# A decoder step on one core: low halves at the bottom of the mix's pool, raw weights in an empty weight place, and rooms of their own for norm and forget values

## The chip, the cores and the metric

One core of a Trainium2 chip. The metric is the device time of one execution in microseconds; each kernel is run several times, and the median counts.

## The reference, cut to what matters

One layer of a hybrid decoder for 512 prompt tokens and 8 sequences of 8 new tokens, D = 1024, all in float32:

```python
mod = einsum('bd,de->be', silu(c), w_ada) + b_ada            # six rows: sh1 sc1 gt1 sh2 sc2 gt2
h = rms_norm(x, norm1_g) * (1 + sc1) + sh1
z = einsum('btd,dc->btc', h, w_in)                           # queries, keys, values, forget, gates mg
...                                                          # two attentions: o_fox, o_nsa
mix = sigmoid(mg_fox) * (o_fox @ w_br_fox) + sigmoid(mg_nsa) * (o_nsa @ w_br_nsa)
x = x + gt1 * (mix @ w_out)
h = rms_norm(x, norm2_g) * (1 + sc2) + sh2
y = x + gt2 * (relu(h @ w_up) ** 2 @ w_down)
```

The forgetting attention adds a difference of summed log forget values to its scores. The sparse attention works on compressed keys, on 16 selected blocks and on a window. For the new tokens, keys, values and log forget values of 2048 past tokens come out of paged caches.

## The kernel before, in words

**Halves.** Each large product is made of three matmuls, high x high, low x high and high x low. `split` (L131) writes the high half with ACT, and the low half as a subtraction on DVE. `stream` (L169 to L184) brings a weight: SP issues the DMA of a raw piece (L179), then the piece is split into its high and low places. With raws=0 the raw piece takes a room of the pool praw, which all such weights share; it has 5 rooms of 4 KB per partition in the program before.

**Stages, in order of time.** The first stage (up to about 166 us) compresses the cached keys and values of the sparse attention in 40 units u, and beside them makes the first norm and the conditioning rows; what is done at which unit is written out by hand in lists (`todo[u]`, L592 ff.). `ada_first` is a conditioning product with a 1 MB weight tile (wada) that POOL loads; `cmp_pages` asks SP for cache pages (cpg); `stage_logf` and `store_logf` gather log forget values and store them again. Then come the projections (to about 305 us), which also leave the normed rows h, split into a high and a low half, in a buffer in DRAM (hfd), the prompt's attention (to about 455 us), the samples' attention (to about 606 us), the mix (to about 768 us), the output projection `out_part` (to about 829 us) and the MLP (8 blocks of an up and a down part).

**Samples' attention** (`sample_attention`, L1554 ff.). 32 units u, four for each sequence. A step of its loop turns the keys of unit u + 1 (`key_rows`: transposes k, then copies kt on ACT and DVE), makes the scores of unit u, and the values (so) of unit u - 3, the key and value rows being fr and sr tiles loaded by SP. forget_split and forget_turned make, once for each sequence, the transposed log forget sums DT out of DH, and E is a constant of selected ones; DH, DT and E stand in the pool sp, which the samples' attention opens when the pools of the prompt's attention close. At u = 24 the high halves hH of all rows are loaded from hfd by POOL. At u = 30 `mix_open` opens praw and asks for the first gate's weights, and in the last steps `mix_first` does the first gate's matmuls with hH. A list that is written out by hand (self.chain) keeps TensorE in program order there and in out_part.

**Mix** (`mix_part`, L1840 to L1916). For each of 8 column blocks e, and for x = 0, 1: a gate mg (8 pieces k of h, two halves of the columns, three matmuls, so 48), its tanh on ACT, and a branch br (4 pieces, 24 matmuls) out of the split attention output oH, oL. Before the first e, two gate results (mg0), oH and oL, the weights of e = 0, and then the low halves hL (16 DMAs on POOL, L1896 and L1897) are taken from the pool pq, in this order from the bottom. Pools give the same memory out again, from the bottom of the stack or, with side="right", from the other end; a tile waits for the last users of what stood at its place. SP then also loads the rows of x2 (L2187).

**Output and MLP.** out_part has four quarters of w_out (wo0 to wo3), each with a place (`place_of`) in pools pwt or pm, and goes through five row tiles i; the norm of a finished row tile (`norm_scaled`, ACT squares, DVE scales it into nsq) is turned by TensorE (`norm_parts`, nt) at a later point of a written-out list (turn_at). gate_prompt and gate_sample make the factors gp and gs. The last row tile's norm is made in mlp, in the room of the accumulator acc. The MLP's w_down halves (wd) use places w3 in pwt, and w0 in its own pool pf; its raw pieces are those of praw.

The order on each engine within what these lists leave open is set by a scheduler (schedule_with_timeline_sim). issue_after pins an instruction behind another in that order.

Of the kernel before, what the change touches and what calls it, by code (L numbers as in the profile page):

```python
# [45 lines left out]
class Step:  # L46
# [121 lines left out]

    def stream(self, pool, src, shape, tag, uid, raws=2, bufs=2, parts=2, room=None, pin=None):  # L169

        nc = self.nc
        wh, wl = room or [pool.tile(shape, F32R, tag=tag + c, bufs=bufs, name=f"{tag}{c}{uid}") for c in "hl"]
        n = shape[1] // parts
        for i in range(parts):
            s = slice(n * i, n * i + n)
            raw = (pool.tile([P, n] + shape[2:], F32, tag=tag + "r", bufs=raws, name=f"{tag}r{uid}_{i}") if raws else
                   self.praw.tile([P, n] + shape[2:], F32, tag="raw", bufs=5, name=f"{tag}r{uid}_{i}"))
            for sl, a in src(s):
                nc.sync.dma_start(raw[sl], a)  # L179
# [331 lines left out]
    def first_stage(self, pl, pe, hf, seam):  # L511
# [182 lines left out]
    def norm_scaled(self, sq, n, i, x, junk=None):  # L694

        t0, m = TILES[i]
        ss = self.small.tile([P, 1], F32, tag="nss", name=f"nss{n}_{i}")
        self.act((sq if junk is None else junk)[:m], x[:m], AF.Square, accum_out=ss[:m])
# [852 lines left out]
    def sample_attention(self, sp, sp0):  # L1551
        nc = self.nc
        self.E = sp.tile([P, 8, 64], F32R, name="E")
        self.tt(self.E, self.tok[:, :, None].to_broadcast([P, 8, 64]), self.hot[:, None, :].to_broadcast([P, 8, 64]), OP.mult)  # L1554
# [13 lines left out]
        for u in range(4 * NB + 4):  # L1568
# [92 lines left out]
    def forget_split(self, sp, b):  # L1661
        self.DH = DH = sp.tile([P, 2, 2, 64], F32R, tag="DH", bufs=1, name=f"DH{b}")
        for hf in range(2):
            d = self.Dt[:, b, 8 * hf:8 * hf + 8, :].rearrange("p c h -> p (c h)")
            self.act(DH[:, hf, 0, :], d)
            self.tt(DH[:, hf, 1, :], d, DH[:, hf, 0, :].bitcast(F32), OP.subtract)

    def forget_turned(self, sp, b):
        tb = self.mmb(f"dt{b}")
        for hf in range(2):  # L1670
            self.tr(tb[:, P * hf:P * hf + P], self.DH[:, hf].rearrange("p a n -> p (a n)").bitcast(F32))
        self.DT[b] = sp.tile([P, 2, P], F32R, tag="DT", bufs=2, name=f"DT{b}")
        self.cp(self.DT[b], tb[:, 0:256].rearrange("p (a n) -> p a n", a=2))
# [154 lines left out]
    def gate_weights(self, e, x):  # L1828
        return self.stream(self.pqr, self.cols(self.I["w_in"], TOK + D * x + P * e, P), [P, NK, P], "wm", f"{x}_{e}", raws=0, parts=1)

# [8 lines left out]

    def mix_part(self, pq, pr, pm, mix2):  # L1840
# [26 lines left out]
        def gate(e, x, w, ks=None):  # L1867
            t = pq.tile([P, NT], F32, tag="mgt", bufs=2, name=f"mgt{e}{x}") if e else mg0[x]
            if e + x == 0:
# [16 lines left out]
        def weights(e, x):  # L1886
            return (self.w0 if e + x == 0 else self.gate_weights(e, x),
                    self.stream(pq, br_src(x, e), [P, 4, P], "wb", f"{x}_{e}", raws=0, parts=1))

        with self.tc.issue_after(self.last_exp):  # L1890
            ws = [weights(0, x) for x in range(2)]

        hL = pq.tile([P, NK, NT], F32R, name="hL2")
        for k in range(NK):

            nc.gpsimd.dma_start(hL[:, k, 0:SEQ], self.hfd[:, k, NT + NS:2 * NT])  # L1896
            nc.gpsimd.dma_start(hL[:, k, SEQ:NT], self.hfd[:, k, NT:NT + NS])  # L1897
        for e in range(NK):
            if e == 0:
                for k in range(8):  # L1900
                    self.split(oH[:, k], oL[:, k], self.oT[:, k])
# [9 lines left out]
            if e == NK - 1:  # L1911
                self.wo0 = self.out_weights(0, self.place_of(0, "wo0", NK, pm))
            (nc.gpsimd if e < NK - 1 else nc.vector).tensor_tensor(m[0], m[0], m[1], op=OP.add)
# [12 lines left out]
    def gate_sample(self, pool, j0, scale, uid, room=None):  # L1926

        gx = room if room is not None else pool.tile([P, NK, NB, 8], F32, tag="gx", bufs=1, name=f"gx{uid}")
        self.cp(gx, self.modT[:, j0:j0 + NK, 1:9, None].to_broadcast([P, NK, NB, 8]))
# [7 lines left out]

    def place_of(self, n, uid, a, pool=None):
# [3 lines left out]
    def out_weights(self, q, room):  # L1942
        return self.stream(None, self.cols(self.I["w_out"], 256 * q, 256), [P, NK, 256], "wo", q, raws=0, room=room)

    def out_part(self, pw, mix2, x2, h3):
        nc, I = self.nc, self.I
        rooms = [self.place_of(q, f"wo{q}", NK) for q in (3, 2, 1)]
        ws = [self.wo0] + [self.out_weights(q, rooms.pop()) for q in range(1, 4)]
        self.shift = self.mod_coef(1)
        g = None  # L1950
        self.chain = ""

        rest, turn_at = {}, {(1, 1): 0, (2, 0): 4, (2, 3): 1, (3, 3): 2}
        for i in (0, 4, 1, 2, 3):
# [17 lines left out]
            if i != 3:  # L1972
                sq = pw.tile([P, D], F32, tag="nsq", bufs=1, name=f"nsq{i}")
                self.norm_scaled(sq, 1, i, x2[:, i])
                rest[i] = lambda i=i, sq=sq: self.norm_parts(i, h3, sq, pw.tile([P, 4, P], F32, tag="nv", bufs=1, name=f"nv{i}"))


    def mlp(self, pf, h3, x2, acc):
# [36 lines left out]

        self.norm_scaled(acc[:, 0], 1, 3, x2[:, 3])
        for blk in range(NBLK):
# [3 lines left out]
            for q in range(2):  # L2021
                v = I["w_down"][0, 512 * blk + 256 * q:512 * blk + 256 * q + 256, :].rearrange("(k p) c -> p k c", p=P)
                w = self.stream(None, lambda s, v=v: [((slice(None),), v[:, s])], [P, 2, D], "wd", f"{blk}{q}",
                                raws=0, room=self.place_of((3, 0)[q], f"wd{blk}{q}", 2, pf if q else None), pin=None if blk else self.normed)
                wd += [(w[0][:, k], w[1][:, k]) for k in range(2)]
# [35 lines left out]
    def run(self):  # L2061
# [46 lines left out]
        lctx.close()  # L2108
        op = self.pool("op2", octx)
        self.Dt = op.tile([P, NB, 16, 8], F32, name="Dt")  # L2110
# [71 lines left out]
        with ExitStack() as c:  # L2182
            c.push(self.mctx)
            self.mix_part(self.pool("pq", c), self.pqr, pm, mix2)
        x2 = keep.tile([P, 5, D], F32, tag="r1", bufs=1, name="x2")
# [5 lines left out]
        h3.append([h31[:, 0], h31[:, 1]])  # L2191
        self.pwt = self.pool("pwt", self.top, side="right")
        with ExitStack() as c:
            self.out_part(self.pool("pw2", c), mix2, x2, h3)
# [46 lines left out]
```

## Time and profile before

| | us |
|---|---|
| median of 3 runs | 1249.14 (1248.99 to 1249.55) |
| profiled execution | 1249.57 |
| span of its profile | 1247.7 |
| TensorE busy (PE) | 1194.9 |
| VectorE (DVE), ScalarE (ACT), GpSimd (POOL) busy | 687.6, 514.2, 127.1 |
| HBM traffic over the span | 166 GB/s |

How to read it: times in the profile are microseconds from the start of the span. A row of the waits names the waiting engine and tile, then what released it, then total, times and longest. A row of a timeline is start, duration, engine, line, operation, out<-in, shape, count, and in brackets the idle time before it and what ended it. A row of the chain is start, duration and what was under way, followed back from the last instruction. A row of windows has the window, its length, busy time and count of instructions in it for PE, its weight loads (PEld), DVE, ACT and POOL, and then the granted TensorE clock, the share of the DMA engines that was busy, and GB/s.

### The profile page before, as it was taken

How to read it: one execution, taken by the hardware profiler on the slowest of the kernel's cores; microseconds unless marked ns; L12 is line 12 of the kernel's file. 1: busy time of each engine (PE TensorE's matmuls, PEld its weight loads, DVE VectorE, ACT ScalarE, POOL GpSimd, SP SyncE). 2: the span in 40 equal slices, each digit the busy share in tenths (PEclk: the TensorE clock that was granted, in tenths of full speed). 3: DMA queues.
4: the chain of work that ended last, by engine and by line, in shares of the span. 5: the costliest groups of instructions: out<-in, count | busy, mean ns of one | idle time of the engine just before them, and what ended most of it. 6: DMA issues, size and time to landing. Idle time of an engine off the chain costs nothing.

```text
span 1247.7 us, 24815 instructions
## 1 busy us (share of the span) xinstructions
PE 1194.9 (96%) x9475; PEld 1024.9 (82%) x9475; DVE 687.6 (55%) x1875; ACT 514.2 (41%) x1152; POOL 127.1 (10%) x142
## 2 busy tenths in 40 slices
PE   3899999999999999999799999999999999999998
PEld 3877789998666556666699999998989889899896
DVE  4678775686788745655444345655333333424545
ACT  2454453454777744445332233365423223232230
POOL 1020100001211300000200000002102011020110
PEclk9999999999999899999899999999999999999999
DMA  9599556794866559786833342115314223142102
GB/s 209 163 259 248 153 151 227 242 321 139 282 225 182 168 191 320 243 276 214 218 87 89 88 119 88 49 52 153 101 34 136 68 69 101 46 124 69 51 1 76
DMA packets 170201, 188.11 MB, mean 151 GB/s; under 512 B 16185, under 2 KB 149762, under 8 KB 167906
## 3 DMA queue, kind: packets, MB, share of 16 engines
q1 hardware_dynamic: 157890, 167.13, 44.5%
q0 software_dynamic: 6880, 16.25, 4.6%
q10 hardware_dynamic: 5312, 3.15, 1.1%
q8 instruction: 75, 1.23, 0.4%
q14 instruction: 44, 0.36, 0.1%
HBM read 176.48 MB, written 30.90 MB: 166 GB/s over the span
## 4 chain that ended last, share of the span: by engine, by line
PE 82%; DMA 7%; DVE 5%; SPq 3%; ACT 2%; issue 1%; POOL 0%; DVEq 0%; ACTq 0%
PE dn L77 17%; PE up L77 16%; PE mg L77 8%; PE z L77 7%; PE br L77 4%; PE hid L77 4%; PE ss L77 4%; PE wo L77 4%; DMA cpg<-in_cache_nsa_kv 4%; SPq L155 2%; PE k L83 2%; PE so L77 2%; PE ct L83 1%; PE sp L83 1%; PE ada L77 1%
## 5 line engine op out<-in xcount | busy, mean ns | idle before, releaser
L77 PE MATMUL z<-winh,h 128*128 128x264 f32 (+1 forms) x576 | 111.0, 287 | 0.6 <-ACT winh L112 0.3
L77 PEld LDWEIGHTS z<-winh,h 128*128 128x128 f32 x576 | 91.7, 190 | 2.7 <-DVE h L774 0.9
L2011 POOL TENSOR_TENSOR u<-u 128x576 f32<-128x576 f32 x32 | 50.7, 1585 | 417.0 <-ACT u L112 319.0
L77 PE MATMUL z<-winl,h 128*128 128x264 f32 (+1 forms) x320 | 88.2, 284 | 0.5 <-DVE winl L131 0.5
L77 PE MATMUL mg<-hL,wmh 128*128 128x288 f32 x256 | 76.0, 309 | 8.0 <-DMA hL<-hfd 8.0
L100 DVE TENSOR_TENSOR acc<-acc,dn 128x512 f32<-128x512 f32 x60 | 39.8, 684 | 76.5 <-PE dn L77 76.5
L77 PE MATMUL mg<-hH,wmh 128*128 128x288 f32 x256 | 76.8, 301 | 0.0
L77 PE MATMUL mg<-hH,wml 128*128 128x288 f32 x256 | 76.0, 298 | 0.6 <-DVE wml L131 0.6
L112 ACT ACTIVATE xh<-ct 128x256 fp32r<-128x256 f32 x128 | 47.9, 384 | 59.0 <-PE ct L83 36.2
L774 DVE TENSOR_TENSOR u<-u,u 128x512 fp32r<-128x512 f32 x64 | 27.2, 469 | 76.5 <-ACT u L112 76.5
L77 PEld LDWEIGHTS z<-winl,h 128*128 128x128 f32 x320 | 60.6, 190 | 0.7 <-DVE winl L131 0.7
L131 DVE TENSOR_TENSOR xl<-ct,xh 128x256 fp32r<-128x256 f32 x128 | 51.3, 420 | 17.8 <-ACT xh L112 16.0
L83 PE MATMUL ct<-identF,ro 128*128 128x128 f32 x256 | 36.2, 280 | 25.1 <-DVE ro L115 21.8
L131 DVE TENSOR_TENSOR wml<-wmr,wmh 128x1024 fp32r<-128x1024 f32 x16 | 19.6, 1224 | 70.9 <-ACT wmh L112 70.8
L77 PEld LDWEIGHTS mg<-hL,wmh 128*128 128x128 f32 x256 | 48.9, 197 | 9.8 <-DMA hL<-hfd 9.7
L112 ACT ACTIVATE u<-up 128x256 f32<-128x256 f32 (+1 forms) x96 | 27.9, 326 | 63.9 <-PE up L77 63.8
L83 PEld LDWEIGHTS ct<-identF,ro 128*128 128x128 f32 x256 | 29.3, 144 | 29.3 <-DVE ro L115 18.4
L77 PEld LDWEIGHTS mg<-hH,wml 128*128 128x128 f32 x256 | 49.5, 193 | 0.8 <-DVE wml L131 0.8
L77 PEld LDWEIGHTS mg<-hH,wmh 128*128 128x128 f32 x256 | 49.0, 192 | 0.2
L77 PE MATMUL hid<-xh,w1hlk 128*128 128x512 f32 (+1 forms) x160 | 44.6, 366 | 0.1
L77 PE MATMUL hid<-xh,w1hlv 128*128 128x512 f32 (+1 forms) x160 | 43.8, 360 | 0.8 <-ACT xh L112 0.5
L112 ACT ACTIVATE mgt<-mg 128x288 f32<-128x288 f32 x32 | 13.0, 409 | 72.0 <-PE mg L77 72.0
(948 smaller groups left out, 3589.1 us busy)
## 6 DMA issues: line engine op xcount, KB each, us to landing
adw<-in_w_ada SPq DMA_DIRECT2D x16, 1024.0 KB
foxD<-in_cache_fox_kv SPq DMA_DIRECT2D x128, 128.0 KB
wur<-in_w_up SPq DMA_DIRECT2D x32, 512.0 KB
wdr<-in_w_down SPq DMA_DIRECT2D x32, 512.0 KB
cpg<-in_cache_nsa_kv SPq DMA_DIRECT2D x120, 128.0 KB
fr<-foxD SPq DMA_DIRECT2D x28, 512.0 KB
sr<-in_cache_nsa_kv SPq DMA_DIRECT2D x112, 128.0 KB
wada<-in_w_ada POOLq DMA_DIRECT2D x8, 1024.0 KB, 7.8
```

The costliest lines, as they stand in the source:

```text
L77: ins = self.nc.tensor.matmul(out, a, b, start=start, stop=stop, skip_group_check=True)
L83: ins = self.nc.tensor.transpose(out, in_, self.identF[:n, :n])
L100: self.nc.vector.tensor_tensor(out, a, b, op=op)
L112: return self.nc.scalar.activation(out, in_, f, **kw)
L131: self.splits.append((eng or self.nc.vector).tensor_tensor(l, x, h.bitcast(F32), op=OP.subtract).ins)
L155: self.issued[eng] = getattr(self.nc, eng).dma_start(out, in_).ins
L774: self.packed = (eng or self.nc.vector).tensor_tensor(h2[:, o:o + n], x[:, i:i + n], h2[:, i:i + n].bitcast(F32), op=OP.subtract).ins
L2011: nc.gpsimd.tensor_tensor(u[j], u[j], u[j], op=OP.mult)
```

## The change

1. In `mix_part` the low halves hL are the first tile of pq, at its bottom, and their 16 DMAs are issued first. The gate results of e = 0 are ordinary mgt tiles.
2. A pool pw0 at the top holds the first weight place w0 (two rooms of 8 KB), which wo0 and the second w_down halves use. Before these come, the raw weights of the first two gates (graw) stand in it. praw has 3 rooms and no longer 5.
3. hH is loaded at u = 26, behind a small POOL copy (late) of the keys of unit 27.
4. E, DH and DT stand in op2, a pool open since the end of the first stage.
5. wo2's raw pieces get two rooms in pw2, and wo3 is pinned behind wo2's splits.
6. The last row tile's norm gets a tile n3 of its own and is made at the end of out_part; the turning of row tile 2 comes behind the last output group.
7. In the first stage the second wada load moves from unit 19 to 23 (behind a small copy), most uses of wada one unit later, two forget rows two units later, and late_loads (small constants) from 19 to 24.

The diff, cut to its core:

```diff
-    def stream(self, pool, src, shape, tag, uid, raws=2, bufs=2, parts=2, room=None, pin=None):
+    def stream(self, pool, src, shape, tag, uid, raws=2, bufs=2, parts=2, room=None, pin=None, raw_at=None):
...
-                   self.praw.tile([P, n] + shape[2:], F32, tag="raw", bufs=5, name=f"{tag}r{uid}_{i}"))
+            raw = (raw_at if raw_at is not None else
+                   pool.tile([P, n] + shape[2:], F32, tag=tag + "r", bufs=raws, name=f"{tag}r{uid}_{i}") if raws else
+                   self.praw.tile([P, n] + shape[2:], F32, tag="raw", bufs=3, name=f"{tag}r{uid}_{i}"))
...
-        todo[19] += [load_x, wada(1), self.late_loads]
+        todo[19] += [load_x]
+        todo[23] += [asked(wada(1))]
+        todo[24] += [self.late_loads]
-        for k, u in enumerate((22, 24, 26, 28, 30, 32, 33, 35)):
+        for k, u in enumerate((22, 25, 27, 29, 31, 32, 34, 35)):
...
-                todo[(23, 25, 27, 29, 31, 33)[k - 2]] += [wada(k)]
+                todo[(23, 26, 28, 30, 32, 33)[k - 2]] += [wada(k)]
...
-        for y, u in enumerate((23, 26)):
+        for y, u in enumerate((25, 28)):
...
-        self.E = sp.tile([P, 8, 64], F32R, name="E")
+        self.E = self.op2.tile([P, 8, 64], F32R, name="E")
...
-            if u == 4 * NB - 8:
+            if u == 4 * NB - 6:
                 self.hH = self.keep.tile([P, NK, NT], F32R, tag="r2", bufs=1, name="hH")
-                self.dma("gpsimd", self.hH, self.hfd[:, :, 0:NT])
+                late = self.small.tile([P, 1], F32, tag="late", bufs=1, name="late")
+                with self.tc.issue_after(nc.gpsimd.tensor_copy(late, self.keys[u + 1][0][:, 0:1]).ins):
+                    self.dma("gpsimd", self.hH, self.hfd[:, :, 0:NT])
...
-        self.DH = DH = sp.tile([P, 2, 2, 64], F32R, tag="DH", bufs=1, name=f"DH{b}")
+        self.DH = DH = self.op2.tile([P, 2, 2, 64], F32R, tag="DH", bufs=1, name=f"DH{b}")
...
-        self.DT[b] = sp.tile([P, 2, P], F32R, tag="DT", bufs=2, name=f"DT{b}")
+        self.DT[b] = self.op2.tile([P, 2, P], F32R, tag="DT", bufs=2, name=f"DT{b}")
...
         self.praw = self.pool("praw", self.top, side="right")
+        self.pw0 = self.pool("pw0", self.top, side="right")
...
-        with self.tc.issue_after(self.last_exp):
-            self.w0 = self.gate_weights(0, 0)
+        self.graw = [self.pw0.tile([P, NK, P], F32, tag="w0", bufs=2, name=f"graw{x}") for x in (1, 0)][::-1]
+        self.w0 = self.gate_weights(0, 0, self.graw[0], (self.last_exp,))
...
-        mg0 = [pq.tile([P, NT], F32, tag="mgt", bufs=2, name=f"mgt0{x}") for x in range(2)]
-        oH, oL = [pq.tile([P, NK, NT], F32R, name=n) for n in ("oH", "oL")]
+        hL, oH, oL = [pq.tile([P, NK, NT], F32R, name=n) for n in ("hL2", "oH", "oL")]
+        for k in range(NK):
+            nc.gpsimd.dma_start(hL[:, k, 0:SEQ], self.hfd[:, k, NT + NS:2 * NT])
+            nc.gpsimd.dma_start(hL[:, k, SEQ:NT], self.hfd[:, k, NT:NT + NS])
...
-        with self.tc.issue_after(self.last_exp):
-            ws = [weights(0, x) for x in range(2)]
-        hL = pq.tile([P, NK, NT], F32R, name="hL2")
-        for k in range(NK):
-            nc.gpsimd.dma_start(hL[:, k, 0:SEQ], self.hfd[:, k, NT + NS:2 * NT])
-            nc.gpsimd.dma_start(hL[:, k, SEQ:NT], self.hfd[:, k, NT:NT + NS])
...
-        return [(pool or self.pwt).tile([P, a, 2048 // a], F32R, tag=f"w{n}", bufs=2, name=f"{uid}{c}") for c in "hl"]
+        return [(self.pwt if n else self.pw0).tile([P, a, 2048 // a], F32R, tag=f"w{n}", bufs=2, name=f"{uid}{c}") for c in "hl"]
...
-        rooms = [self.place_of(q, f"wo{q}", NK) for q in (3, 2, 1)]
-        ws = [self.wo0] + [self.out_weights(q, rooms.pop()) for q in range(1, 4)]
+        ws = [self.wo0, self.out_weights(1), self.out_weights(2, pw)]
+        ws += [self.out_weights(3, pin=(self.splits[-1], self.last_high))]
...
-        rest, turn_at = {}, {(1, 1): 0, (2, 0): 4, (2, 3): 1, (3, 3): 2}
+        rest, turn_at = {}, {(1, 1): 0, (2, 0): 4, (2, 3): 1}
...
+        self.norm_scaled(self.n3, 1, 3, x2[:, 3])
+        with self.tc.issue_after(self.squares):
+            rest.pop(2)()
...
-                            self.norm_parts(3, h3, acc[:, 0], acc[:, 1, 0:SEQ].rearrange("p (k t) -> p k t", k=4))
+                            self.norm_parts(3, h3, self.n3, acc[:, 1, 0:SEQ].rearrange("p (k t) -> p k t", k=4))
...
-        self.norm_scaled(acc[:, 0], 1, 3, x2[:, 3])
```

More of the change, by code (lines that the diff above doesn't have):

```diff
@@ L697, in norm_scaled @@
         ss = self.small.tile([P, 1], F32, tag="nss", name=f"nss{n}_{i}")
[L698 removed]
+        self.squares = self.act((sq if junk is None else junk)[:m], x[:m], AF.Square, accum_out=ss[:m]).ins
         rs = self.small.tile([P, 1], F32, tag="nrs", name=f"nrs{n}_{i}")
@@ L1867, in gate @@
         def gate(e, x, w, ks=None):
-            t = pq.tile([P, NT], F32, tag="mgt", bufs=2, name=f"mgt{e}{x}") if e else mg0[x]
+            t = pq.tile([P, NT], F32, tag="mgt", bufs=2, name=f"mgt{e}{x}")
             if e + x == 0:
@@ L1886, in weights @@
         def weights(e, x):
-            return (self.w0 if e + x == 0 else self.gate_weights(e, x),
-                    self.stream(pq, br_src(x, e), [P, 4, P], "wb", f"{x}_{e}", raws=0, parts=1))
-        with self.tc.issue_after(self.last_exp):
-            ws = [weights(0, x) for x in range(2)]
-        hL = pq.tile([P, NK, NT], F32R, name="hL2")
-        for k in range(NK):
-            nc.gpsimd.dma_start(hL[:, k, 0:SEQ], self.hfd[:, k, NT + NS:2 * NT])
-            nc.gpsimd.dma_start(hL[:, k, SEQ:NT], self.hfd[:, k, NT:NT + NS])
+            pin = None if e else (self.last_exp,)
+            return (self.w0 if e + x == 0 else self.gate_weights(e, x, None if e else self.graw[x], pin),
+                    self.stream(pq, br_src(x, e), [P, 4, P], "wb", f"{x}_{e}", raws=0, parts=1, pin=pin))
         for e in range(NK):
             if e == 0:
+                ws = [weights(0, x) for x in range(2)]
                 for k in range(8):
@@ L1926, in gate_sample @@
     def gate_sample(self, pool, j0, scale, uid, room=None):
-        gx = room if room is not None else pool.tile([P, NK, NB, 8], F32, tag="gx", bufs=1, name=f"gx{uid}")
+        gx = room if room is not None else pool.tile([P, 4, P], F32, tag="nv", bufs=1, name=f"gx{uid}").rearrange(
+            "p a (b c t) -> p (a b) c t", c=NB, t=8)
         self.cp(gx, self.modT[:, j0:j0 + NK, 1:9, None].to_broadcast([P, NK, NB, 8]))
@@ L2023, in mlp @@
                 w = self.stream(None, lambda s, v=v: [((slice(None),), v[:, s])], [P, 2, D], "wd", f"{blk}{q}",
-                                raws=0, room=self.place_of((3, 0)[q], f"wd{blk}{q}", 2, pf if q else None), pin=None if blk else self.normed)
+                                raws=0, room=self.place_of((3, 0)[q], f"wd{blk}{q}", 2), pin=None if blk else self.normed)
                 wd += [(w[0][:, k], w[1][:, k]) for k in range(2)]
@@ L2108, in run @@
         lctx.close()
-        op = self.pool("op2", octx)
+        op = self.op2 = self.pool("op2", octx)
         self.Dt = op.tile([P, NB, 16, 8], F32, name="Dt")
@@ L2183, in run @@
             c.push(self.mctx)
-            self.mix_part(self.pool("pq", c), self.pqr, pm, mix2)
+            self.mix_part(self.pool("pq", c), self.pqr, mix2)
         x2 = keep.tile([P, 5, D], F32, tag="r1", bufs=1, name="x2")
@@ L2192, in run @@
         self.pwt = self.pool("pwt", self.top, side="right")
+        self.n3 = self.pool("pn3", self.top, side="right").tile([P, D], F32, name="n3")
         with ExitStack() as c:
```

17 lines of the change are left out of this document (9 added, 8 removed).

## The prediction

> **What bounds the kernel now.** First the page: span and busy time of each engine.
>
> ```profile
> span 1247.7 us, 24815 instructions
> ...
> PE 1194.9 (96%) x9475; PEld 1024.9 (82%) x9475; DVE 687.6 (55%) x1875; ACT 514.2 (41%) x1152; POOL 127.1 (10%) x142
> ```
>
> TensorE is busy for 96% of the span. So a gain can only come out of its 1247.7 - 1194.9 = 52.8 us of idle time, or out of work done at a lowered clock: nothing in the diff removes a matmul. I therefore read next whom TensorE waited for (total, times, longest), and keep the rows that the diff touches.
>
> ```profile
> PE mg L77 <- DMA hL<-hfd: 8.0, 6, 3.7
> PE ct L83 <- DVE nrs L109: 2.8, 1, 2.8
> PE dt L83 <- DVE DH L100: 1.8, 1, 1.8
> PE nt L83 <- DVE nsq L104: 1.8, 1, 1.8
> PE wk L83 <- DMA wr<-in_state_win_kv: 1.2, 1, 1.2
> ```
>
> These five sum to 15.6 us; the largest stands at the seam from the samples' attention to the mix. Here is that seam in the chain of waits, and one window of it (after the busy times of the engines: granted clock, DMA share, GB/s).
>
> ```profile
> 605.78 0.43 DVE oT L115
> ...
> 606.29 0.56 POOL hL L1896
> ...
> 616.41 9.30 DMA hL<-hfd
> ...
> 627.27 7.50 PE br L77 x48
> 634.77 6.37 PE mg L77 x48
> 641.14 3.18 PE br L77 x24
> ```
> ```profile
> 612.00:614.00 2.00, 1.58 (x6) 1.58 (x7) 1.09 (x2) 0.00 (x0) 1.07 (x2) 0.50 1.28 288
> ```
>
> The low halves hL are asked for only at 606.29, behind the attention's last output (oT, 605.78), and the first two gates run at the pace at which they land. The waits cost more than their 8.0 us: the clock granted in the window is 0.50, and the 48 branch matmuls behind them take 7.50, where twice the steady 3.18 would be 6.36.
>
> **The change part by part.**
>
> *A. Low halves at the bottom of the pool.* At 605.78 these matmuls are left of the first e: 16 of gate 0 (those with hL; its 32 others ran early, in mix_first), 48 of gate 1, and 48 of the branches. By the steady rows (48 in 6.37) one steps on in 0.1325 us. At full clock without waits that is 64 x 0.1325 = 8.5, then 48 x 0.1325 = 6.4: the second e would start at 605.8 + 14.9 = 620.7 and not at 634.77, a gain of 14.1 us. Will hL be there? Its new place is that of attention tiles whose last readers come early. Of the waits that the changed program puts on the first hL DMA, the last in time is the maximum of the last score group, first row; the second is hL's own landing, from the view of one tile.
>
> ```profile
> 595.11 0.08 DVE L1694 DVE_READ_ACCUMULATOR2_ANT ss<- 128x1 f32 x1
> ```
> ```profile
> DMA to landing us min/median/max: 2.7/6.5/9.4
> ```
>
> Issued from 595.2 and not 606.29, that is 11.1 us earlier. 16 DMAs at the 0.56 of the POOL row are out by 604.2, and even with the worst landing the last is there at 613.6; its piece, k = 7, is needed after 7/8 of the 8.5 us, at 613.2. With the median landing there are 2.5 us to spare. Behind POOL's wait stands only hL itself. The branches start at 614.3; they need oT's splits, which ACT and DVE can do in these 8.5 us, since nothing else is due on them. I take **-14.0**; ends -10 (two waits of the sizes seen, with half clock behind one) and -14.1.
>
> *B. First gates' raw weights in the first weight place.* In the changed program the first gate's DMA waits for the values of unit 27, in the program before for those of unit 25.
>
> ```profile
> 590.71 0.23 PE L77 MATMUL so<-sr,spT 128*32 128x64 f32 x2
> ```
> ```profile
> 582.74 0.40 SPq L179 DMA_DIRECT2D wmr<-in_w_in  x1
> ```
> ```profile
> 590.07 1.05 ACT L112 ACTIVATE wmh<-wmr 128x1024 fp32r<-128x1024 f32 x1
> ```
> ```profile
> 595.38 0.38 PE L77 MATMUL mg<-hH,wmh 128*128 128x288 f32 x1
> 596.39 0.40 PE L77 MATMUL mg<-hH,wml 128*128 128x288 f32 x1 [0.62 <-DVE wml L131]
> ```
>
> So it is asked for at about 591.0, 8.3 us later. If it lands in 2.7, as the quickest hL did, the high copy (1.05) ends at 594.8; with 3.5, at 595.6; it is used at 595.38. The DVE subtraction already held TensorE for 0.62 and comes little later. Behind this DMA on SP are queued the branches' raws and the second gate's, all used 2 us or more after; behind the copy on ACT, the weights of unit 29, which wait for transposes of about 595.4 anyway. **+0.3**; ends 0 and +3.
>
> *C. High halves hH two units later, on POOL behind a copy of unit 27's keys.*
>
> ```profile
> 519.27 0.96 POOL L155 DMA_DIRECT2D hH<-hfd  x1 [78.17 <-PE so L77]
> ```
> ```profile
> 534.04 0.66 PE L83 MATMUL wk<-identF,wr 128*128 128x128 f32 x4 [1.25 <-DMA wr<-in_state_win_kv]
> ```
> ```profile
> 578.00:582.00 4.00, 4.00 (x69) 2.74 (x57) 2.27 (x14) 3.38 (x11) 0.00 (x0) 1.00 0.16 52
> ```
>
> It was issued at 519.27, though nothing reads it before 595.38, and it lands among window rows for which TensorE then waits. After the change it goes out near 572 by the order of the units, with the last units' keys; soon after, at 578 to 582, the DMA share is only 0.16, so there is room for it. Behind its copy on POOL stands only hL. **-1.25**; ends 0 (the wait comes back at the last keys) and -1.3.
>
> *D. E, DH and DT in op2.* They no longer wait for the prompt's pools to close, so forget_split and E run beside the prompt's attention.
>
> ```profile
> 455.54 0.67 PE L83 MATMUL dt<-identF,DH 128*128 128x128 f32 x2 [1.84 <-DVE DH L100]
> 456.00 1.91 PE L83 MATMUL k<-identF,rows 128*128 128x128 f32 x8
> ```
> ```profile
> 456.00:458.00 2.00, 2.00 (x11) 1.67 (x12) 2.00 (x11) 1.00 (x3) 0.00 (x0) 0.50 0.89 331
> ```
>
> The wait is 1.84, and behind it 8 transposes take 1.91 at a clock of 0.50, so half of it, 1.0, is lost, and some 0.6 at the score matmuls behind them. Without the wait that is 3.4. Next late is the copy of the first keys, on ACT behind the second pair of DH copies, which wait for dt: about 1.3 of TensorE's time by the durations of these copies (my estimate from 1.05 for a copy twice as wide, and the transposes' 0.67). **-2.0**; ends -0.5 (the clock falls behind the new wait too) and -2.6. One rule of the Trainium skill speaks against half of this term: TensorE: Matmul & The Clock Gate, section HAM oscillation, has the clock fall behind idle gaps of more than about 3.4 us, so that a wait of 1.84 would cost no clock, and the term would be 0.5. The window with 0.50 behind that wait differs from it, and I go by the window.
>
> *E. Last norm in a room of its own.* The transposes of row tile 2 (the nt row of the waits, 1.8) go behind the last output group, whose matmuls are ready and cover the wait; the last tile's norm starts before the MLP opens its pool. **-1.8**; ends -1 and -1.9.
>
> *F. Output weights.* The third's raw data (wo2) take rooms of pw2 in hL's old place, so their DMA waits for the last hL matmul of the mix, and the gate factors gp go ahead of their split on ACT.
>
> ```profile
> 772.21 1.99 ACT L112 ACTIVATE wo2h<-wor 128x1024 fp32r<-128x1024 f32 x2
> ...
> 775.06 1.06 ACT L112 ACTIVATE gp<-gp 128x512 f32<-128x512 f32 x2
> ```
>
> Seven e of 19.1 from 634.77 end the mix at 768.5, its hL matmuls one branch (3.18) earlier, at 765.3; with landings of 3 to 6 the raws are there at 768 to 771, before 772.21. With gp's 1.06 ahead, the high parts end near 775.3, about when the third quarter's matmuls come. SP has the fourth quarter and the MLP's first raws queued behind; they are needed later. **+0.5**; ends 0 and +1.5.
>
> *G. Three shared raw rooms for five.* In the mix four pieces are used per 2 x (6.37 + 3.18) = 19.1 us, one in 4.8; three rooms leave about 10 us from a room's release to the use of what it gets next, against landings of 2.7 to 9.4. The rows of x2 now pass SP ahead of the second e's last branch weights; these are used 15 us later. **0**, covered by that slack; the slower rival prices its loss.
>
> *H. First stage: a conditioning weight (wada) is asked for later, its users one step later, the forget rows two.*
>
> ```profile
> 78.98 0.90 POOL L155 DMA_DIRECT2D wada<-in_w_ada  x1
> ```
> ```profile
> 94.62 0.69 DVE L115 COPY ro<-cpg 128x1024 f32<-128x1024 f32 x1 [3.95 <-DMA cpg<-in_cache_nsa_kv]
> ```
> ```profile
> 92.00:96.00 4.00, 1.15 (x13) 0.94 (x10) 1.38 (x4) 1.04 (x3) 0.92 (x1) 1.00 0.81 206
> ```
>
> TensorE's 2.8 us, put down to nrs, stand behind DVE's wait for cache pages, 3.95. A load of 1 MB, issued at 78.98, ran ahead of those pages; at the window's 206 GB/s it is 5 us of DMA time, more than the wait. Moved behind them, it is asked for at about 93 and used two units (some 10 us) later; POOL's later wada loads and forget rows queue behind. **-2.5**; ends -2.85 (with what follows nrs) and +2 (wada late by a little).
>
> **Sum**: -14.0 + 0.3 - 1.25 - 2.0 - 1.8 + 0.5 + 0 - 2.5 = -20.75. The profiled execution took 1249.57 (1.9 of it outside its span), so 1228.8. It stands 0.43 above the median of the runs, 1249.14.
>
> **Rivals.**
> - *The gates' weights come late instead.* TensorE waits at mix_first for graw0: 3 us from B, and as much again if the clock halves as at 612. 1232 to 1235. For it: 8.3 us of lead are gone. Against: the DMA had been almost idle before (0.16). Chance 0.11.
> - *hL lands late anyway*: 2.4 MB of hL and 2 MB of weights from 591 on. At 288 GB/s that is 15 us, done by 606; at half of that it is 621, 8 us late, and A shrinks to about -5. 1238. Chance 0.10.
> - *The change doesn't do what it says*: the place is not free earlier, because another wait of the first hL DMA ends as late as oT. A is 0, the rest stays. 1242.8. Chance 0.06.
> - *Slower: three raw rooms starve the MLP.* The place is the start of each of its 8 blocks, where four pieces are split one right after another.
>
> ```profile
> 931.75 2.01 ACT L112 ACTIVATE wd20h<-wdr 128x1024 fp32r<-128x1024 f32 x2 [19.75 <-PE dn L77]
> ```
> ```profile
> 958.31 1.86 PE dn L77 x8
> ```
>
> With three rooms the fourth piece can be asked for only when the first has been read, near 934, and is split at 939 to 945 with landings of 2.7 to 9.4; the matmuls that use it start at 958.31. It decides only from 13 us of further lateness on; then each block would pay 3 and as much at half clock, about 45 us in all: 1274. Chance 0.07.
>
> **How the numbers follow.** The forecast, 1225 to 1232, has the remaining 0.66. The ends of all terms together reach from 1226 to above 1244. I give 1225 to 1241: outside lie the slower rival (0.07), most of the third (0.05) and a larger gain than I can name (0.05). A difference of 0.2%, 2.5 us, is about what a measurement of this kernel can tell from no change. Faster by more than that holds in all cases but the slower one and the tail of the third: 0.90; within it 0.03; slower 0.07.
>
> **What would show it.** By the mix all is some 6 us earlier. A: hL issued near 589, no wait of mg for hL, a granted clock of 1.0 through the seam, some 15 us from the attention's end to the second e. B: at most 1 us of wait at the first mg. C, D, E, H: the rows wk, dt, nt and nrs gone from TensorE's waits, and a clock of 1.0 behind dt. F: a new wait of wo, under 1.5. G: no wait for wmr, wbr, wur or wdr. It is wrong if mg still waits for hL, or if new waits (graw0, wada, the first keys, wo) add up to more than 4 us.

## The result, and the profile after

The changed kernel takes 1229.95 us (median of 4 runs, 1227.63 to 1231.71), the one before 1249.07 (4 runs, 1246.85 to 1249.55): ratio 0.985, 95% interval 0.983 to 0.987. The forecast was 1228.8. The profiled execution took 1231.5, with a span of 1229.7; so 18.0 us of span went. First the page of the changed kernel: span and busy time.

```profile
span 1229.7 us, 24815 instructions
...
PE 1186.9 (97%) x9475; PEld 1022.7 (83%) x9475; DVE 684.9 (56%) x1875; ACT 513.6 (42%) x1152; POOL 131.2 (11%) x144
```

TensorE's idle time fell from 52.8 to 42.8, and its busy time by 8.0 with the same 9475 matmuls, so these ran faster; a better clock is only a part of that. Whom TensorE waited for (total, times, longest), the rows that belong to the stages touched:

```profile
PE wk L83 <- DMA wr<-in_state_win_kv: 2.6, 2, 2.2
PE mg L77 <- ACT wmh L112: 2.0, 1, 2.0
...
PE k L83 <- ACT kt L112: 1.0, 1, 1.0
PE mg L77 <- DVE wml L131: 0.9, 1, 0.9
```

The rows of hL (8.0), nrs (2.8), dt (1.8) and nt (1.8) are gone. The row wr, which was to go, has grown from 1.2 to 2.6, and the first gate's weights (wmh and wml) hold TensorE for 2.9, where at most 1 was forecast. Totals don't say what a wait costs, so I measured the length of each stretch between two markers on TensorE (first or last matmul of a kind) in both profiles. All figures are us of span.

| stretch of TensorE's work | before | after | change | predicted |
|---|---|---|---|---|
| start to first ada | 91.0 | 91.5 | +0.5 | |
| first stage, first ada to first z | 82.0 | 79.3 | -2.7 | H -2.5 |
| projections, first to last z | 129.3 | 127.9 | -1.4 | |
| prompt's attention | 147.2 | 147.7 | +0.5 | |
| its end to the first samples' score | 8.4 | 6.5 | -1.9 | D -2.0 |
| first score to the first values (first so that reads rows) | 12.8 | 16.2 | +3.4 | |
| first values to last score | 122.7 | 121.8 | -0.9 | C -1.25 |
| last score to end of the samples' attention | 12.2 | 16.2 | +4.0 | B +0.3 |
| from there to the last mg with hL (the mix) | 159.4 | 145.2 | -14.2 | A -14.0 |
| to the last wo of the third quarter | 58.2 | 59.2 | +1.0 | F +0.5 |
| to the first up that reads h (those of the last rows, h3, start earlier) | 17.3 | 15.4 | -1.9 | E -1.8 |
| MLP | 407.3 | 402.7 | -4.6 | G 0 |

So the total is right by more than its terms deserve: +3.4, +4.0 and -4.6 were not foreseen and cancel down to +2.8. That is luck: without the -4.6 the changed kernel would stand near 1234.5 (pad_after below, which lacks it, took 1233.64), above the 1225 to 1232 of the forecast's own case. Where the three come from is shown in what follows. The seam to the mix in the chain of waits (start, duration, what was under way):

```profile
588.74 5.50 DMA graw<-in_w_in
594.24 0.02 issue
594.26 1.06 ACT wmh L112
595.33 0.02 issue
595.35 1.24 DVE wml L131
...
607.47 7.76 PE mg L77 x57
...
615.78 6.63 PE br L77 x48
622.41 6.35 PE mg L77 x48
```

The chain now goes through the first gate's weights and no longer through hL: from 607.47 on it is TensorE alone, and the second e starts at 622.41 (before 634.77). The loads of hL on POOL, the first and the ninth:

```profile
593.69 0.56 POOL L1856 DMA_DIRECT2D hL<-hfd  x1 [22.57 <-PE sp L83]
...
601.61 0.54 POOL L1856 DMA_DIRECT2D hL<-hfd  x1 [3.64 <-DMA hL<-hfd]
```

They go out from 593.69 (606.29 before), with one pause of 3.64. And the windows of the seam (length, busy times of five engines, granted clock, DMA share, GB/s):

```profile
594.00:596.00 2.00, 0.40 (x1) 0.19 (x1) 0.65 (x1) 1.54 (x2) 2.00 (x5) 1.00 1.22 263
596.00:598.00 2.00, 1.37 (x11) 1.09 (x15) 1.28 (x6) 1.01 (x3) 1.97 (x4) 0.88 1.24 248
598.00:600.00 2.00, 2.00 (x37) 1.83 (x38) 0.16 (x1) 1.98 (x6) 0.00 (x0) 0.50 1.37 327
...
606.00:614.00 8.00, 8.00 (x69) 7.54 (x69) 6.48 (x11) 5.23 (x9) 0.00 (x0) 1.00 0.62 152
```

From 606 to 614, where TensorE worked for 3.87 of 8 us before, it is full at a clock of 1.00. The price stands ten microseconds earlier: waits at 594 to 597, then a clock of 0.50.

### The profile page after: what moved, and what is told of

Read it like the earlier page. It is cut to its first block, busy times and chain, and to the rows that moved or that the text cites. A ratio compares the mean times of both kernels' runs of the same rounds, so it can differ in the third digit from the quotient of the medians.

```text
span 1229.7 us, 24815 instructions
## 1 busy us (share of the span) xinstructions
PE 1186.9 (97%) x9475; PEld 1022.7 (83%) x9475; DVE 684.9 (56%) x1875; ACT 513.6 (42%) x1152; POOL 131.2 (11%) x144
## 4 chain that ended last, share of the span: by engine, by line
PE 85%; DVE 5%; DMA 4%; SPq 3%; ACT 2%; issue 1%; DVEq 0%; ACTq 0%
PE up L77 17%; PE dn L77 17%; PE mg L77 8%; PE z L77 7%; PE hid L77 5%; PE wo L77 4%; PE br L77 4%; PE ss L77 4%; SPq L155 3%; PE k L83 2%; PE ct L83 2%; PE so L77 2%; DMA cpg<-in_cache_nsa_kv 2%; PE ada L77 1%; PE sp L83 1%
## 5 line engine op out<-in xcount | busy, mean ns | idle before, releaser
L2024 POOL TENSOR_TENSOR u<-u 128x576 f32<-128x576 f32 x32 | 53.4, 1669 | 409.3 <-ACT u L112 318.2
L112 ACT ACTIVATE xh<-ct 128x256 fp32r<-128x256 f32 x128 | 48.0, 385 | 59.2 <-PE ct L83 35.8
L77 PE MATMUL mg<-hL,wmh 128*128 128x288 f32 x256 | 72.6, 294 | 0.0
L83 PE MATMUL ct<-identF,ro 128*128 128x128 f32 x256 | 36.3, 281 | 22.7 <-DVE ro L115 22.1
L131 DVE TENSOR_TENSOR wml<-wmr,wmh 128x1024 fp32r<-128x1024 f32 x14 | 17.1, 1224 | 56.0 <-ACT wmh L112 55.9
L1700 DVE CUSTOM_DVE_ANT_0 sS<-ss,scr 128x512 f32<-128x512 f32 x32 | 22.1, 691 | 30.2 <-PE ss L77 30.2
```

Of the source, the lines that this page charges most:

```text
L77: ins = self.nc.tensor.matmul(out, a, b, start=start, stop=stop, skip_group_check=True)
L83: ins = self.nc.tensor.transpose(out, in_, self.identF[:n, :n])
L112: return self.nc.scalar.activation(out, in_, f, **kw)
L131: self.splits.append((eng or self.nc.vector).tensor_tensor(l, x, h.bitcast(F32), op=OP.subtract).ins)
L1700: self.nc.vector.tensor_tensor_reduce(self.S[u], pb, self.ramp[:, 512 * i:512 * i + 512], 1.0, LOW, OP.add, OP.max, self.stat[b][0][:, i / ...
L2024: nc.gpsimd.tensor_tensor(u[j], u[j], u[j], op=OP.mult)
```

## The experiments

Twelve more runs were made, one of them of the changed kernel again (after_again) and one a repeat (mixed_again). The kernel before ran beside each of them, and the ratios are to it. Stretches and waits below are each from one profiled execution.

**Where do 4.6 us of the MLP come from?** The change touches two things there: three raw rooms for five, and the places of the tiles. One theory has it that nothing but the places counts. *pad_before* is the kernel before with a tile of 4 bytes more in the pool at the bottom, which moves what stands above it by 32 bytes, and a copy that nobody waits for. The change's own tile late (part 3) moves the same tiles in the same way.

```diff
             if u == 4 * NB - 8:
...
+                late = self.small.tile([P, 1], F32, tag="late", bufs=1, name="late")
+                nc.gpsimd.tensor_copy(late, self.keys[u + 1][0][:, 0:1])
```

> The kernel before with one tile of 4 bytes more per partition in the small pool (and a POOL copy of one column that nothing waits for); it moves every tile above by 32 bytes, as the change's own 4-byte tile does. The down blocks of the MLP, 25.97 us each before, took 25.39 after. Theory 1, placement alone: here too they take about 25.4, 8 x 0.58 = 4.6 us less, 1244.5 in all, and nothing else moves. Theory 2, the weights' new pool (w_down's second halves in pw0) did it: the blocks stay at 25.97 and the time at 1249.

It took 1243.90 (10 runs, 1240.41 to 1250.57) against 1248.56 (20 runs), ratio 0.997 (0.995 to 0.9996). In the chain of waits the second down block (112 matmuls in a row) of the kernel before, of the changed one, and of pad_before:

```profile
906.91 25.97 PE dn L77 x112
```
```profile
892.95 25.39 PE dn L77 x112
```
```profile
903.84 25.39 PE dn L77 x112
```

The same 112 matmuls take 0.58 less, and so it is in every block that the chain shows; 8 x 0.58 = 4.6. pad_before has nothing of the change but a tile of that size, and shows all of it: its MLP takes 402.7, as in the changed kernel. By groups (busy time, mean ns of one) it is the matmul itself and no wait; the first row is the kernel before, the second the changed one:

```profile
L77 PE MATMUL dn<-wd10h,u 128*128 128x512 f32 x36 | 11.6, 395 | 0.0
```
```profile
L77 PE MATMUL dn<-wd10h,u 128*128 128x512 f32 x36 | 11.4, 389 | 0.0
```

*pad_after* puts one more such tile (late2) into the changed kernel.

> The changed kernel with one more such tile, so that the same tiles start 32 bytes further still and stand to multiples of 64 bytes as in the kernel before. Theory 1: the down blocks go back to about 25.9 to 26.0 and the time rises by 4 to 5 us against the changed kernel, to about 1235. Theory 2: blocks at 25.39 and no change, 1230.

1233.64 (4 runs, 1232.97 to 1235.67), ratio 0.989 (0.986 to 0.991), 3.7 above the changed kernel's median; its down block, in the chain of waits:

```profile
889.36 26.12 PE dn L77 x112
```

So the gain is taken away again by 32 bytes (its MLP takes 408.5). To see which operand's place counts, *right_after* and *right_pad* move the tiles at the other end of the stack (weights wd among them), in the changed kernel and in pad_after:

```diff
+        nc = self.nc
+        nc.gpsimd.memset(self.pool("rpad", self.top, side="right").tile([P, 8], F32, name="rpad"), 0.0)
         self.praw = self.pool("praw", self.top, side="right")
```

> The changed kernel with 32 bytes more at the other end of the memory: the weight places (wd, wo, wu) and h3 now start at multiples of 64 bytes, while u2 and mix stay 32 bytes behind one. Theory 1, the down blocks are quick only where wd and u2 have the same offset to 64 bytes (both 32 in the changed kernel): 25.9 to 26.1 us here, 4 to 6 us slower than the changed kernel, 1235. Theory 2, u2's offset alone decides: 25.39 and 1230.

> Both shifts: wd and u2 all at multiples of 64 bytes. Theory 1, same offset: blocks at 25.4, 1230. Theory 2, u2 at a multiple of 64 is slow by itself: 26.0 to 26.1, 1235. In between, near 25.8, if the high and the low parts count apart, as the durations of the second halves in the kernel before (394 and 390 ns) may say.

right_after took 1234.99 (1232.06 to 1235.67), ratio 0.989 (0.986 to 0.992), and right_pad 1235.25 (1232.04 to 1236.19), ratio 0.989 (0.986 to 0.992). Their down blocks took 26.13 each, their up blocks 25.33 (25.44 in all other kernels). First right_after, then right_pad, in the chain of waits:

```profile
892.10 26.13 PE dn L77 x112
```
```profile
893.11 26.13 PE dn L77 x112
```

By the addresses in the built programs, the offsets of weights and values (wd, u) to a multiple of 64 bytes are 32 and 32 where a block takes 25.39, and 32/0, 0/32 and 0/0 where it takes 26.12 to 26.13; in the kernel before, with 25.97, half of the weights are at 32 and the rest at 0, the values at 0. Neither "both at the same offset" nor "the values alone" fits all four. "Both at 32" does, but it does not say why the kernel before, with all values at 0, is quicker than the three slow ones. It is shown that places alone move the block by 0.58 to 0.74 us; what in the address does it stays open.

**Is the early place what lets hL start early?** *low_first* is the kernel before with hL as first tile of pq and its DMAs first, and nothing else:

```diff
+        hL, oH, oL = [pq.tile([P, NK, NT], F32R, name=n) for n in ("hL2", "oH", "oL")]
+        for k in range(NK):
+            nc.gpsimd.dma_start(hL[:, k, 0:SEQ], self.hfd[:, k, NT + NS:2 * NT])
+            nc.gpsimd.dma_start(hL[:, k, SEQ:NT], self.hfd[:, k, NT:NT + NS])
         mg0 = [pq.tile([P, NT], F32, tag="mgt", bufs=2, name=f"mgt0{x}") for x in range(2)]
-        oH, oL = [pq.tile([P, NK, NT], F32R, name=n) for n in ("oH", "oL")]
...
-        hL = pq.tile([P, NK, NT], F32R, name="hL2")
...
```

> The kernel before with the low halves hL as first tile of their pool and their DMAs issued first, nothing else. Theory 1, part A is worth its 14 us alone: no wait of mg for hL, second e some 14.8 us behind the attention's end in place of 28.9, 1235. Rival, the first DMA waits here for unit 31's values and the last prompt output, so it is asked for some 8 us later than in the changed kernel: hL comes at the pace of the DMA, about half of the 8.0 us of waits stays, 1241 to 1243.

1240.59 (5 runs, 1239.96 to 1241.63), ratio 0.994 (0.992 to 0.996). The first load on POOL, then the wait in the table of waits:

```profile
602.11 0.56 POOL L1846 DMA_DIRECT2D hL<-hfd  x1 [85.69 <-PE so L77]
```
```profile
PE mg L77 <- DMA hL<-hfd: 3.1, 5, 0.9
```

The order alone moves the load from 606.29 to 602.11 only: the bottom of that pool is free there only when values (so) of the attention's last units are made. The mix's stretch is 150.2, 9.2 less than before; the changed kernel's 145.2. So 9 of the 14 come with the order alone. The other 5 go with an earlier release of that place: in the changed kernel the last thing that the load waits for is sp, before 593.69. By the addresses in the built programs this is the work of part 2: the two rooms of w0 no longer stand below pq, its bottom lies 16 KB lower, and of the last four units' rows hL covers only fr of unit 28, in low_first fr of all four and sr of unit 28. No run has parts 1 and 2 alone; undo_forget and place_first below keep 145.1 and 145.2, so it is neither part 4 nor the order of the pools at the top.

**Which part gives the first stage its 2.7?** *first_stage* is the kernel before with part 7 of the change alone (the todo lists in the diff).

> The kernel before with the new first stage alone (second wada load at unit 23, its users one unit later, forget rows two). Theory 1: the 2.85 us of waiting for cache pages near 92 us go, the projections start 2.0 to 2.7 us earlier, 1246.5; if the later weights of the projections also land earlier, as they did by 0.9 in the changed kernel, 1245.5. Rival: the wait only moves to the pages or wada loads behind it, 1249.

1246.53 (10 runs, 1242.64 to 1249.59), ratio 0.9975 (0.996 to 0.999). First ada to first z takes 79.4 (79.3 in the changed kernel), and no wait for nrs is left. The late load costs nothing: in the changed kernel wada goes out at 94.91 (about 93 was forecast), and nobody waits for it.

**Are the 4.0 us at the first gate the late weights?** *place_first* is the changed kernel with two lines exchanged, so that the raw weights come to stand over the rows of an earlier unit:

```diff
-        self.praw = self.pool("praw", self.top, side="right")
         self.pw0 = self.pool("pw0", self.top, side="right")
+        self.praw = self.pool("praw", self.top, side="right")
```

> The changed kernel with the pools pw0 and praw opened in the other order: the first gate's raw weights then stand over the rows of unit 24 and no longer over those of unit 27. Theory 1, the wait of 1.96 us for wmh, that for wml and the half clock of 597.5 to 601 all come from the late load: graw0 is asked for near 578, no wait above 0.7 at the first mg, from the last maximum to the attention's end 10.8 us in place of 14.6: 3.5 to 3.9 us faster than the changed kernel, 1226.2. Rival, DMA and ACT are late there anyway because of hL's DMAs: under 1 us of gain.

1227.03 (4 runs, 1225.15 to 1230.17), ratio 0.983 (0.979 to 0.986). The load on SP, then the first gate's matmuls that waited, from two timelines of this kernel:

```profile
578.91 0.40 SPq L180 DMA_DIRECT2D graw<-in_w_in  x1
```
```profile
596.81 0.40 PE L77 MATMUL mg<-hH,wml 128*128 128x288 f32 x1 [0.63 <-DVE wml L131]
```

And the same matmuls of the changed kernel:

```profile
595.37 0.40 PE L77 MATMUL mg<-hH,wmh 128*128 128x288 f32 x1 [1.96 <-ACT wmh L112]
596.63 0.40 PE L77 MATMUL mg<-hH,wml 128*128 128x288 f32 x1 [0.86 <-DVE wml L131]
```

Asked for 9.8 us earlier, the weights are there. The wait for the high part is gone, the wait for the low part is that of the kernel before, and the stretch is 12.2 again, from 16.2. So all 4.0 hang on the release of the place. The medians differ by 2.9 only, with the runs of both kernels overlapping.

**What does part 4 (E, DH, DT) bring?** *undo_forget* is the changed kernel with these three tiles back in the pool sp, so that `self.op2.tile` is `sp.tile` in three lines.

> The changed kernel with E, DH and DT back in the pool sp. Theory 1, the 5 KB in op2 push the prompt's tiles up under the samples' first rows, so that their loads wait for the prompt's last outputs: here the rows of units 2 and 3 are asked for before 447 us again, the wait of 2.2 us for window rows and the half clock behind it go (3.4 us), the wait for DH comes back (2.0 us): 1.4 us faster than the changed kernel, 1228.5. Rival, the window rows come late because the attention starts earlier than the DMA can follow: the wait for them shrinks only by as much as dt is later, and the time is within 0.5 us of the changed kernel's or slower.

1229.67 (4 runs, 1226.63 to 1230.64), ratio 0.985 (0.981 to 0.988): no difference from the changed kernel that can be told, where 1.4 less was expected. Where the part took and gave, from SP's timelines, first the rows sr of unit 2 and, last, the window rows (wr) in the kernel before:

```profile
432.93 2.24 SPq L155 DMA_DIRECT2D sr<-in_cache_nsa_kv  x4
...
450.23 0.90 SPq L155 DMA_DIRECT2D wr<-in_state_win_kv  x2
```

the same in the changed kernel,

```profile
445.95 1.93 SPq L155 DMA_DIRECT2D sr<-in_cache_nsa_kv  x4
...
453.88 0.90 SPq L155 DMA_DIRECT2D wr<-in_state_win_kv  x2
```

and in undo_forget:

```profile
430.86 2.24 SPq L155 DMA_DIRECT2D sr<-in_cache_nsa_kv  x4
...
448.19 0.90 SPq L155 DMA_DIRECT2D wr<-in_state_win_kv  x2
```

With 5 KB more in op2 the prompt's pools above it stand 5 KB higher, while the samples' rows keep their places; so one of these row tiles lies over a tile that the prompt uses nearly to its end. By the addresses in the built programs it is sr of unit 2: it lies over factors of the prompt's outputs (Ffox), in the kernel before and in undo_forget over sums (cS, cP) that are done with earlier. Its load goes out 13 us later, and in SP's order the window rows stand behind it and come 3.65 later. TensorE waits for them, in its timeline of the changed kernel (the first row is the wait that was forecast):

```profile
452.01 1.09 PE L83 MATMUL k<-identF,rows 128*128 128x128 f32 x8 [0.98 <-ACT kt L112]
...
460.35 0.66 PE L83 MATMUL wk<-identF,wr 128*128 128x128 f32 x4 [2.19 <-DMA wr<-in_state_win_kv]
```

From the prompt's end to the first values the changed kernel takes 22.7, undo_forget 21.2, the kernel before 21.2. The 22.7 is the worst of its kind: in the six other profiles with part 4, after_again among them, it is 20.3 to 22.3, and in all those without it 19.6 to 21.2. So in the profiles the part costs rather than gives, by about 1.

**Both undone.** *mixed* is place_first and undo_forget in one.

> Both: E, DH and DT back in sp, and pw0 opened before praw. If both theories hold the gains add up, 1.4 + 3.7 = 5.1 us: 1224.9. If the wait for DH costs as much as the late rows, 1226.

1223.95 (4 runs, 1222.34 to 1226.24), ratio 0.9815 (0.978 to 0.985). It was run once more beside the changed kernel, on one chip, as *mixed_again* and *after_again*.

> The changed kernel once more, beside the next one on the same chip: 1230, and the waits for window rows (1 to 2 us) and for wmh (1 to 2 us) again.

> The changed kernel with E, DH and DT back in sp and pw0 opened before praw, once more: 4 to 6 us below the changed kernel beside it, if both theories hold; under 2 us, if the earlier gain lay between chips.

after_again: 1230.22 (5 runs, 1229.6 to 1231.86), ratio 0.986 (0.983 to 0.9885). mixed_again: 1225.42 (5 runs, 1224.76 to 1227.24), ratio 0.982 (0.980 to 0.985). The medians lie 4.8 us apart, and no run of the one falls among those of the other. place_first and mixed differ by part 4 alone: mixed, without it, is 3.1 below, with the runs overlapping by 1.1. What is left of the waits in mixed_again:

```profile
PE dt L83 <- DVE DH L100: 1.8, 1, 1.8
...
PE mg L77 <- DVE wml L131: 0.6, 1, 0.6
...
PE wk L83 <- DMA wr<-in_state_win_kv: 0.5, 2, 0.3
```

The wait of dt is back, and the kernel is the fastest of all. The same wait of 1.84 stands in seven of the profiles, and the clock behind it differs. The two microseconds behind the end of that wait, first in the kernel before, then in mixed_again:

```profile
455.54:457.54 2.00, 2.00 (x10) 1.98 (x10) 2.00 (x14) 0.84 (x3) 0.00 (x0) 0.51 0.90 313
```
```profile
452.69:454.69 2.00, 2.00 (x14) 1.41 (x15) 2.00 (x14) 1.00 (x3) 0.00 (x0) 1.00 0.87 291
```

In before, first_stage and undo_forget it fell to half, and from the prompt's end to the first values took 21.1 to 21.2; in pad_before, low_first, mixed and mixed_again it stayed at 1.00, and the stretch took 19.6. So that clock costs 1.6, and it does not come each time.

**Does hH have to come two units later?** *high_24* is the changed kernel with hH at u = 24 again, behind the copy of the keys of unit 25.

```diff
-            if u == 4 * NB - 6:
+            if u == 4 * NB - 8:
```

> The changed kernel with hH loaded at unit 24 in place of 26, behind the same kind of copy (of the keys of unit 25). Theory 1, the load was in the way of rows that TensorE waits for wherever it stands among the loads of the units: a wait of about 1 us for rows returns at some unit after it, 1230.5 to 1231.5. Rival, behind the copy it is late enough at either place: no wait and 1230.

1228.74 (4 runs, 1228.06 to 1229.07), ratio 0.985 (0.981 to 0.988): no loss. hH went out at 562.80, in the changed kernel at 570.16, and in the kernel before, without a copy ahead of it, at 519.27. First values to last score took 121.6 (121.8 changed, 122.7 before). So it is the copy that holds the load back, and 44 us of lateness do as well as 51. Whether the lateness itself is worth anything is another question, and undo_forget speaks against it. There hH goes out at 570.13, and TensorE waits for window rows at 531.81 all the same (the row of the waits; 1.25 in the kernel before):

```profile
PE wk L83 <- DMA wr<-in_state_win_kv: 1.1, 1, 1.1
```

## Why the prediction was right, and where it was not

- **A, -14.0: right, -14.2.** The reason held too: hL out of the way of the attention's last output, no wait of mg for it, clock 1.00 from 606 to 614. Its first DMA went out at 593.69, about 5 later than forecast on the new time axis: 3.4 of that is D's second step, and 0.7 comes because not the maximum of the last scores but a transposition behind it (sp) released the load. low_first shows that the order of the tiles alone gives 9 of it; the other 5 need w0 out from below the pool, which the prediction did not name.
- **B, +0.3: wrong, +4.0.** The step that failed is "if it lands in 2.7, ... with 3.5". The landing took 5.50. 2.7 was the quickest landing of another tile; its median, 6.5, stood in the same row. In the six other profiles with this place it took 4.49 to 5.06. The windows of the changed kernel from its issue on:

```profile
588.00:590.00 2.00, 2.00 (x93) 1.48 (x89) 0.75 (x4) 0.00 (x0) 0.00 (x0) 1.00 0.12 19
590.00:592.00 2.00, 2.00 (x16) 0.92 (x13) 1.21 (x3) 0.00 (x0) 0.00 (x0) 1.00 0.99 253
592.00:594.00 2.00, 1.41 (x40) 1.00 (x38) 0.70 (x2) 0.00 (x0) 0.31 (x1) 1.00 1.16 217
```

  The DMAs were idle until 590 (share 0.12), as the case against the rival had it; but the loads that SP issues right behind this one share them from 590 on (0.99, 1.16). That they stretched the landing is likely and not tested alone; hL, issued at 593.69, came too late to do it. Behind the waits of 1.96 and 0.86 came the half clock. So the rival that the forecast gave 0.11 is what happened here, at +4.0 of its +3 to +6; the time stayed in the forecast because the MLP made up for it. In after_again the wait was 1.11 and the stretch 15.4, in high_24 13.8; so the term is 1.6 to 4.
- **C, -1.25: the size about right, -0.9, the reason not shown.** The wait fell from 1.25 to 0.46, but in undo_forget, with hH as late, it is 1.08. No run loads hH early in the changed kernel; over all profiles the waits for window rows in this stretch add up to 0.8 to 2.0 with the early load and 0 to 1.1 with the late one, so the two ranges meet. What makes the load late is the copy ahead of it, not the two units.
- **D, -2.0: right where it looked, wrong as a whole.** The new wait is 0.98 where I had 1.3, the clock behind it 1.00, and the stretch is 1.9 shorter. But I counted what three tiles in op2 release and not what they push: 3.4 were lost right behind it, with the window rows (1.8 in after_again, where the wait was 1.72 and the clock stayed at 1.00). Besides, of the 3.4 that I put on the old wait, the 1.6 of clock are lost in some profiles and not in others. undo_forget says that in sum the part is worth nothing that can be measured; the other profiles, and mixed against place_first, put it rather at a loss.
- **The rule weighed at D.** The Trainium skill, TensorE: Matmul & The Clock Gate, section HAM oscillation, puts the limit for idle gaps at about 3.4 us. The runs differ from it: half clock behind waits of 1.84 (three of seven) and 2.19 (the window below). By that rule none of these would have cost clock. But going by one window was wrong as well: a single profile can't price this.

```profile
462.00:464.00 2.00, 2.00 (x11) 0.65 (x9) 0.00 (x1) 0.00 (x0) 0.00 (x0) 0.50 1.00 370
```

- **E, -1.8: right, -1.9.** The row nt is gone from the waits; no run undoes this part alone. **H, -2.5: right, -2.7**, shown alone by first_stage.
- **F, +0.5: the size about right, the reason not.** TensorE's longest wait there is 0.2 (wo for mix), none is for wo2. The stretch is 59.2, but pad_before, which has none of F's edits, also shows 58.9 (58.2 before). So up to 0.7 of the 1.0 may go with the tiles' places; right_pad, which has F's edits, shows 57.8.
- **G, 0: right.** TensorE waited for no raw piece in the MLP, so the slower rival did not come. The MLP's -4.6 came from elsewhere, and no term had it.
- **Not explained:** projections -1.4. This stretch was 127.5 to 129.3 in all kernels, with no relation to their edits, and the prompt's attention 146.3 to 149.8.
- **The sign of being wrong** that the prediction set, more than 4 us of new waits, was all but met: wmh, wml and the first keys make 1.96 + 0.86 + 0.98 = 3.8, and the window rows' 2.19, which its list left out, would bring it to 6.0.

In sum: the predicted part (A, C, E, H and D's first step) was put at 21.6 and came as 21.6. B and D's second step took 7.1 more than forecast, the places in the MLP gave 4.6, and the rest (start, projections, prompt's attention, F) nearly nothing.

## What to carry to other kernels

A tile that is moved to a lower pool pushes all that stands above it: besides what it releases, look up which late-used tiles come to lie under which early loads, and which loads queue behind those. A load is priced with the median landing of loads like it, with those that will run beside it, and not with the quickest. And before a gain in an untouched stage is credited to an edit, a kernel that only shifts the tiles by the same bytes shows how much of it is placement. A gain read from one pair of profiles wants a second profile: with part 4 unchanged, the first wait for window rows ran from 0.50 (right_after) to 2.19 us (the changed kernel).

## What the runs showed of the hardware

The pace of matmuls depends on where their operands stand: 32 bytes make a block of 112 (128x512) take 25.39 or 26.12 us, and one of 192 (up) 25.33 or 25.44. The clock behind one and the same wait of 1.84 us was half in three profiles and full in four; behind 1.72 (wk in after_again) it stayed at 1.00, behind 1.82 at the same place (high_24) it fell to 0.50. A load of 512 KB (graw) took 4.49 to 5.50 us to land in seven profiles, though in the changed kernel the DMAs had been nearly idle (0.12) when it was issued.
